# Operand sums taken pair by pair and one bank for the first half's products, in the output projection of a two-layer decoder

## The chip, the cores and the metric

The kernel runs on one core of a Trainium2 chip. The metric is the device time of one execution in microseconds. Each engine works through its own list of instructions in order. In the profile PE is TensorE's matmuls (PEld its weight loads), DVE is VectorE, ACT is ScalarE, POOL is GpSimd and SP is SyncE.

## The reference, cut to what matters

A batch of one, 512 tokens, a width of 1024. Layer 0 mixes with gated linear attention, layer 1 with stick-breaking attention over 16 heads of 64; each mixer and each MLP (1024 to 4096 to 1024, squared ReLU) is followed by a layer norm of `ALPHA * h + result`. All is float32. The change lies in layer 1's mixer:

```python
k, v  = split(h @ kv_w);  q = h @ sb_w_q[0]
# per head and block of 128 queries, strictly causal:
z     = q @ k.T * 64 ** -0.5
w     = sigmoid(z) * product of (1 - sigmoid(z)) over the keys between
o     = w @ v                        # 512 x 1024 over all heads
mix   = o @ sb_w_o[0]                # the output projection, 1024 x 1024
h     = layer_norm(ALPHA * h + mix)  # then MLP, then layer norm
```

## The kernel before, in words

**Precision.** A float32 operand X is split into `hi` (X rounded to fp32r, a copy on ScalarE) and `lo` (X minus hi, a subtract: the "lo split"). A product is three matmuls: hi·hi, hi·lo, lo·hi. `split_tile` (L70, L72) splits a 128x1024 weight tile, `put` (L98, L99) an activation. `on=nc.gpsimd` sends a lo split to GpSimd; without it VectorE makes it. `raw`, `d`, `k` and `q` are buffers that weight tiles arrive in; `unit()` gives a 128 x 4 x 512 tile, in the profile `T`.

**Layer 1.** The heads go by pairs, eight of them. While pair p's weights are turned (`turn`: transposes at L973, ScalarE copies `wt` at L978), the queries of pair p+1 (`queries`, L927 and L928) and the keys of pair p+2 are projected; then come pair p+1's `weights` (scores at L939, mask at L956, sigmoids at L960 and L961, a reversed scan on VectorE at L964), then pair p's `outputs` (L987: 28 matmuls over `wt` and the values `vs`, into one PSUM bank). The scan's result needs the values as differences of neighbouring rows: `differences(n)` makes them for half n of the heads, by shifted DMA copies and four VectorE subtracts (L904). `vs[0]` serves pairs 0 to 3.

**The output projection.** o is cut in four blocks: columns of pairs 0 to 3 are `o1` (T_5008 in the order lists), those of pairs 4 to 7 `o2`; each has two halves of 256 tokens, a11 and a21 (of `o1`), a12 and a22 (of `o2`). The product is made with seven products instead of eight, in a scheme of operand sums: `first` takes a11, `seventh` a11 - a21, `sixth` and `fifth` sums with a22, `third` a sum with a12, and b2 and b4 are multiplied with parts of `o2` itself (`o2h`, `o2l`). b1 to b7 are the blocks of `sb_w_o` and sums of them, the sums made by accumulating DMAs (`fetch`, L1009). Each product is two half-products (s = 0, 1), each 12 matmuls on one PSUM bank (L1035), and `add` reads a finished bank into the residual rows: four row tiles `h` (in the order lists h_1637 to h_1640) of two 512-wide halves; L167 is the first read of such a half (it scales h by ALPHA), L169 any later one. The first product and half of the seventh run while pair 7's weights are turned; the rest, `project()`, after pair 7's outputs. `finish` then takes the layer norm's statistics of each row tile as it is complete (L177, L182 to L184, L190), transposes it (L231) and splits it (L98, L99) for the first matmuls of the MLP (L93 to L95, there 256 wide).

**What sets the order.** Code order and priorities, through a scheduler; `keep_in_program_order` (`keep`) pins an instruction against others that are pinned on its engine. A tile's buffer is handed on when its last reader is through.

## Time and profile before

| | us |
|---|---|
| median of three runs (lowest, highest) | 1122.48 (1121.60, 1123.09) |
| the profiled execution's own time | 1122.67 |
| its span in the trace, 0.998 granted clock | 1121.0 |
| busy: PE, DVE, ACT, POOL | 1104.7, 822.5, 571.7, 159.3 |

The 1.67 us between span and execution's time lie outside the trace. A timeline row gives start, duration, engine, line, operation and tile, a count and, in brackets, how long the engine had been idle before and what ended that. The durations of neighbours overlap a little, so the pace of a run is read from the distance of two starts. Attention lies at about 600 to 741 us of the span, the rest of the output projection at 741 to 781, the second MLP from there to the end.

### The profile page before, as it was taken

The numbers are of one execution on the slowest core, as the hardware profiler recorded it, in microseconds if no ns is written. First come the engines' busy times: TensorE is split into PE (matmuls) and PEld (weight loads), VectorE is DVE, ScalarE is ACT, GpSimd is POOL, SyncE is SP. The second block draws the span as 40 slices with busy tenths as digits, with TensorE's granted clock in tenths as the row PEclk, the third lists the DMA queues.
The fourth block names the chain that finished last, engine by engine and source line by source line (L and its number), as shares of the span: only waits on it lengthen the run. The fifth ranks groups of instructions, "written<-read, shape, count | busy, mean of one in ns | idle before, by whom it ended". The sixth has DMA issues, their size and how long they took to land.

```text
span 1121.0 us, 14387 instructions
## 1 busy us (share of the span) xinstructions
PE 1104.7 (99%) x5503; PEld 914.5 (82%) x5503; DVE 822.5 (73%) x1028; ACT 571.7 (51%) x855; POOL 159.3 (14%) x183
## 2 busy tenths in 40 slices
PE   9999999999999999999999999988999999999997
PEld 7888888898888888888888787767988888888885
DVE  4588649958957856849898877698479767667677
ACT  4455437643533534535765667665545435336353
POOL 1011222200100100122313000251200000000222
PEclk9999999999999999999999999999999999999999
DMA  8441399492670760888745352414926815706773
GB/s 248 121 132 57 119 257 207 126 298 84 199 210 22 197 198 19 220 190 169 216 107 170 94 149 78 104 34 126 313 82 191 241 57 164 229 21 187 174 133 89
DMA packets 111352, 169.06 MB, mean 151 GB/s; under 512 B 13178, under 2 KB 38138, under 8 KB 111284
## 3 DMA queue, kind: packets, MB, share of 16 engines
q1 hardware_dynamic: 86228, 119.39, 32.7%
q0 software_dynamic: 22592, 44.04, 22.6%
q10 hardware_dynamic: 2464, 4.72, 1.1%
q8 instruction: 43, 0.70, 0.2%
q14 instruction: 25, 0.20, 0.1%
HBM read 162.89 MB, written 3.15 MB: 148 GB/s over the span
## 4 chain that ended last, share of the span: by engine, by line
PE 90%; DVE 6%; ACT 1%; issue 1%; POOL 0%; POOLq 0%; DVEq 0%; ACTq 0%
PE ps L355 29%; PE ps L93 17%; PE ps L94 17%; PE ps L95 17%; PE ps L796 3%; DVE lo L72 1%; PE ps L939 1%; PE ps L973 1%; DVE c L964 1%; DVE T L99 1%; PE ps L987 1%; DVE h L169 1%; PE ps L231 1%; DVE bst L177 1%; DVE h L167 0%
## 5 line engine op out<-in xcount | busy, mean ns | idle before, releaser
L355 PE MATMUL ps<-hi,T 128*128 128x512 f32 x1008 | 313.3, 390 | 0.1
L93 PE MATMUL ps<-T,hi 128*128 128x512 f32 (+1 forms) x776 | 290.7, 375 | 0.0
L94 PE MATMUL ps<-T,hi 128*128 128x512 f32 (+1 forms) x776 | 287.9, 371 | 2.2 <-DVE T L99 2.1
L95 PE MATMUL ps<-T,lo 128*128 128x512 f32 (+1 forms) x776 | 287.7, 371 | 0.0
L70 ACT ACTIVATE hi<-raw 128x1024 fp32r<-128x1024 f32 x128 | 135.5, 1061 | 169.4 <-PE ps L355 59.6
L72 DVE TENSOR_TENSOR lo<-raw,hi 128x1024 fp32r<-128x1024 f32 x125 | 151.8, 1221 | 95.2 <-ACT hi L70 94.9
L355 PEld LDWEIGHTS ps<-hi,T 128*128 128x128 f32 x1008 | 188.9, 188 | 40.1 <-DVE T L99 0.6
L70 ACT ACTIVATE hi<-B 128x1024 fp32r<-128x1024 f32 x118 | 124.4, 1059 | 172.0 <-PE ps L94 107.3
L72 DVE TENSOR_TENSOR lo<-B,hi 128x1024 fp32r<-128x1024 f32 x118 | 142.9, 1221 | 87.6 <-ACT hi L70 87.6
L355 PE MATMUL ps<-lo,T 128*128 128x512 f32 x504 | 196.1, 389 | 0.0
L94 PEld LDWEIGHTS ps<-T,hi 128*128 128x128 f32 x776 | 147.1, 190 | 26.0 <-DVE T L99 2.7
L95 PEld LDWEIGHTS ps<-T,lo 128*128 128x128 f32 x776 | 146.9, 189 | 24.8
L93 PEld LDWEIGHTS ps<-T,hi 128*128 128x128 f32 x776 | 146.7, 189 | 24.4 <-issue 1.0
L314 POOL DMA_DIRECT2D B<-in_mlp_w_down_dram x52 | 62.9, 1257 | 542.8 <-DMA B<-in_mlp_w_down_dram 386.7
L355 PEld LDWEIGHTS ps<-lo,T 128*128 128x128 f32 x504 | 94.6, 188 | 19.5
L169 DVE TENSOR_TENSOR h<-h,ps 128x512 f32<-128x512 f32 x114 | 77.3, 681 | 2.6 <-PE ps L355 2.2
L99 DVE TENSOR_TENSOR T<-s,T 128x1024 fp32r<-128x1024 f32 (+1 forms) x52 | 54.7, 1054 | 10.6 <-ACT T L98 10.6
L98 ACT ACTIVATE T<-s 128x1024 fp32r<-128x1024 f32 (+1 forms) x52 | 48.4, 935 | 21.2 <-DVE s L721 14.1
L964 DVE TENSOR_TENSOR_SCAN c<-r,c 128x384 f32<-128x384 f32 (+2 forms) x64 | 49.8, 829 | 3.5 <-ACT c L961 3.4
L93 PE MATMUL ps<-hi,T 128*128 128x512 f32 x128 | 51.4, 402 | 0.0
L719 ACT ACTIVATE s<-ps 128x512 f32<-128x512 f32 x64 | 38.0, 594 | 25.9 <-PE ps L95 25.2
L95 PE MATMUL ps<-hi,T 128*128 128x512 f32 x128 | 50.3, 393 | 0.0
(212 smaller groups left out, 1310.4 us busy)
## 6 DMA issues: line engine op xcount, KB each, us to landing
raw<-in_mlp_w_up_dram SPq DMA_DIRECT2D x64, 512.0 KB, 5.5
B<-in_mlp_w_down_dram SPq DMA_DIRECT2D x64, 512.0 KB, 5.6
B<-in_mlp_w_down_dram POOLq DMA_DIRECT2D x52, 512.0 KB, 7.8
raw<-in_gla_w_in_dram SPq DMA_DIRECT2D x20, 512.0 KB, 3.6
raw<-in_mlp_w_down_dram SPq DMA_DIRECT2D x16, 512.0 KB, 4.7
B<-in_gla_w_o_dram POOLq DMA_DIRECT2D x14, 512.0 KB, 7.8
raw<-in_kv_w_dram SPq DMA_DIRECT2D x12, 512.0 KB, 4.6
B<-in_gla_w_o_dram SPq DMA_DIRECT2D x8, 512.0 KB, 6.3
```

Of the source, the lines that this page charges most:

```text
L70: keep(nc.scalar.activation(hi, raw, AF.Copy))
L72: keep((on or nc.vector).tensor_tensor(lo, raw, hi.bitcast(F32), op=ALU.subtract))
L93: keep(nc.tensor.matmul(ps, lhsT=a[0], rhs=b[0], start=first, stop=False))
L94: keep(nc.tensor.matmul(ps, lhsT=a[0], rhs=b[1], start=False, stop=False))
L95: keep(nc.tensor.matmul(ps, lhsT=a[1], rhs=b[0], start=False, stop=last))
L98: keep(nc.scalar.activation(hi, ps, AF.Copy))
L99: keep((on or nc.vector).tensor_tensor(lo, ps, hi.bitcast(F32), op=ALU.subtract))
L169: nc.vector.tensor_tensor(h, h, ps, op=op)
L314: nc.gpsimd.dma_start(out=b.rearrange("p (a b) -> p a b", a=2), in_=weights(k, h, j), accum_op=ALU.add)
L355: nc.tensor.matmul(banks[s], lhsT=a(k, s)[x], rhs=b[k][y], start=opens and (k, x, y) == (0, 0, 0), stop=closes and (k, x, y) == (3, 1, 0), ...
L719: nc.scalar.activation(s2[:, f, :], pss[f], AF.Relu)
L964: nc.vector.tensor_tensor_scan(down, r[:, at][:, ::-1], down, 0.0, op0=ALU.mult, op1=ALU.add)
```

## The change

1. `differences(0)` issues the shifted copies as before, and hands back a function that issues the four subtracts; it is called after pair 1's queries.
2. The operand sums are made as each pair's output comes: `less` is a11 - a21 for all four pairs of `o1`, made after pair 3. Then `sums(k, o)` makes, from the PSUM bank of pair 4, 5 and 7 (from the copy in `o2` for pair 6), a21 as the difference o[HI] - a21 and a11 from it and `less`: two 128x256 operations on VectorE. The seventh operand is split from `less` in one go. The first two units of `o2h` are copied in pair 7's turn, and their lo part is made behind it.
3. `add` finds out itself whether a row half is read for the first time. First, sixth, fifth and third product are summed on one bank for each s (`ys`), the seventh and b4 on another (`us`), b2 on a third (`xs`): each s has 7 reads by VectorE where it had 10.
4. Of the lo splits and sums on GpSimd (b2, b6's first, b5's first, b3's first, `sixth`, `fifth`, `less(most)`) only the two of b2 stay there; the others are on VectorE, or gone.

The diff, cut to its core:

```diff
--- before.py
+++ after.py
...
             nc.gpsimd.dma_start(out=shifted[t][P - 1:P, :], in_=v[P - 2:P - 1, t, :])
             if t:
                 nc.gpsimd.dma_start(out=shifted[t][0:1, :], in_=v[P - 1:P, t - 1, :])
-        for t in range(NT):
-            nc.vector.tensor_tensor(v[:, t, :], v[:, t, :], shifted[t], op=ALU.subtract)
+
+        def subtract(keep=lambda ins: ins):
+            for t in range(NT):
+                keep(nc.vector.tensor_tensor(v[:, t, :], v[:, t, :], shifted[t], op=ALU.subtract))
+
+        return subtract
...
-    def add(s, banks, i, j, first=False, last=False, **how):
-        hs[2 * i + s].add(j, banks[s], first, last, ALU.subtract if j else ALU.add, **how)
+    seen = set()
+
+    def add(s, banks, i, j, last=False, **how):
+        hs[2 * i + s].add(j, banks[s], (i, j, s) not in seen, last, ALU.subtract if j else ALU.add, **how)
+        seen.add((i, j, s))
...
-    differences(0)
+    subtract = differences(0)
     ALL = [(j, j, NT) for j in range(NT)]
     pool = dict(on=nc.gpsimd)
-    ys, us, xs, zs, ws = ([None, None] for _ in range(5))
-    most, rest = slice(0, 3), slice(3, 4)
-
-    def less(ks, eng):
-        eng.tensor_tensor(a22[:, ks, :], a22[:, ks, :], a21[:, ks, :], op=ALU.subtract)
-
-    def flip(ks):
-        return minus(a11[:, ks, :], a22[:, ks, :], a11[:, ks, :])
+    ys, us, xs = ([None, None] for _ in range(3))
+    full = slice(0, 4)
+
+    def sums(k, o):
+        tt(a21[:, k, :], o[:, HI], a21[:, k, :], op=ALU.subtract)
+        minus(a11[:, k, :], o[:, HI], less[:, k, :])
 
     for p in range(NP):
         made = pairs[p].turn()
         take = lambda at: lambda n: [next(made, None) for _ in range(at.get(n, 0))]
         if p + 2 < NP:
             pairs[p + 1].queries()
-            if 0 < p < NT:
+            if p == 0:
+                subtract(keep)
+            elif p < NT:
                 hs[p].affine(vec, keep)
             pairs[p + 2].keys(take(TAKE))
         elif p + 1 < NP:
             pairs[p + 1].queries(take(FILL))
         else:
             mid = take(FILLS)
+
+            def then(n):
+                mid(n)
+                if n == 11:
+                    keep(nc.scalar.activation(o2h[:, 0:2, :], o2[:, 0:2, :], AF.Copy))
+
             run(STEPS, halves(first), b1, ys, closes=False, mid=mid)
-            run(STEPS[:4], halves(seventh), b7, us, mid=lambda n: mid(8 + n))
+            run(STEPS[:4], halves(seventh), b7, us, closes=False, mid=lambda n: then(8 + n))
         for _ in made:
             pass
-        if p == NP - 2:
-            o2h, o2l = unit(F32R), unit(F32R)
-            put(o2h[:, 0:2, :], o2l[:, 0:2, :], o2[:, 0:2, :], keep)
         if p < NP - 2:
             pairs[p + 1].weights()
             if p == 1:
-                differences(1)
-            ops = pairs[p].outputs(ALL)
-        else:
-            ops = pairs[p].outputs(LAST)
+                differences(1)()
+        if p == NP - 1:
+            tt(o2l[:, 0:2, :], o2[:, 0:2, :], o2h[:, 0:2, :].bitcast(F32), op=ALU.subtract)
+            put(o2h[:, 2, :], o2l[:, 2, :], o2[:, 2, :], keep)
+            sums(2, o2[:, 2, :])
+            for s in range(2):
+                add(s, ys, 0, 0)
+        ops = pairs[p].outputs(ALL if p < NP - 2 else LAST)
...
                 o2 = unit(F32)
                 a12, a22 = o2[:, :, LO], o2[:, :, HI]
-            if p < NP - 2:
-                nc.scalar.activation(o2[:, p - 4, :], ops, AF.Copy)
+            if p == NP - 1:
+                put(o2h[:, 3, :], o2l[:, 3, :], ops)
+            if p != NP - 2:
+                sums(p - 4, ops)
+            nc.scalar.activation(o2[:, p - 4, :], ops, AF.Copy)
+        if p == 3:
+            first = unit(F32R)
+            into(first, a11, full)
+            less = sbp.tile([P, 4, 256], F32, name="less")
+            tt(less, a11, a21, op=ALU.subtract)
...
             pairs[p + 1].weights()
-            less(most, nc.gpsimd)
-            keep(flip(most))
...
-            seventh = unit(F32R)
-            for h in range(2):
-                ks, sub = slice(2 * h, 2 * h + 2), chain().rearrange("p (a b) -> p a b", a=2)
-                tt(sub, a11[:, ks, :], a21[:, ks, :], op=ALU.subtract)
-                put(seventh[:, ks, LO], seventh[:, ks, HI], sub)
...
-    ahead_of = lambda u, a, ks: keep(nc.scalar.activation(u[:, ks, LO], a[:, ks, :], AF.Copy))
-
-    ahead_of(sixth, a11, most)
-    for s in range(2):
-        for i, j in ((0, 1), (1, 0), (1, 1)):
-            add(s, ys, i, j, True, keep=keep)
-    nc.gpsimd.tensor_tensor(sixth[:, most, HI], a11[:, most, :], sixth[:, most, LO].bitcast(F32), op=ALU.subtract)
...
-    into(sixth, a11, rest)
-    b6 += parts(b22[1])
-    into(fifth, a22, slice(0, 4), **pool)
-    for j in range(2):
-        add(0, us, 1, j)
+            seventh, o2h, o2l = unit(F32R), unit(F32R), unit(F32R)
+            into(seventh, less, full)
+
+    b6 = pieces(b22)
+    sixth, fifth = unit(F32R), unit(F32R)
+    into(sixth, a11, full)
+    into(fifth, a21, full)
...
-        run(LATER, whole(0), b2, ys, opens=False)
+        run(LATER, whole(0), b2, xs)
         for s in range(2):
-            add(s, ys, 0, 0, True, True)
+            add(s, xs, 0, 0, last=True)
+        b5s = pieces(b5)
+        run(STEPS, halves(sixth), b6, ys, False, False)
+        for s in range(2):
+            add(s, ys, 1, 0)
         minus(a12, a12, a11)
-        b5s = parts(b5[0], **pool) + parts(b5[1])
-        run(STEPS, halves(sixth), b6, zs, closes=False)
-        for s in range(2):
-            add(s, zs, 1, 0)
         third = unit(F32R)
-        into(third, a12, slice(0, 4))
-        run(STEPS, halves(fifth), b5s, zs, False, False)
-        add(0, zs, 1, 1, last=True)
-        add(1, zs, 1, 1)
-        b3 = pieces_512(sb_w_o[0], 512, 2, 512, **pool) + pieces_512(sb_w_o[0], 768, 2, 512)
+        into(third, a12, full)
+        add(0, us, 1, 1)
+        b3 = pieces_512(sb_w_o[0], 512, 4, 512)
+        run(STEPS, halves(fifth), b5s, ys, False, False)
+        add(0, ys, 1, 1, last=True)
+        add(1, ys, 1, 1)
         b4 = pieces(b22)
         for s in range(2):
-            run(STEPS[4 * s:4 * s + 4], halves(third), b3, zs, False)
-            add(s, zs, 0, 1, last=True)
+            run(STEPS[4 * s:4 * s + 4], halves(third), b3, ys, False)
+            add(s, ys, 0, 1, last=True)
             yield s
-        up0.extend(pieces_512(mlp_w_up[1], 0, 4, 0, keep=keep))
-        run(STEPS[4:], halves(seventh), b7, us)
+        up0.extend(pieces_512(mlp_w_up[1], 0, 2, 0, keep=keep))
+        run(STEPS[4:], halves(seventh), b7, us, closes=False)
         add(1, us, 1, 1, last=True)
-        add(1, us, 1, 0)
         yield ~0
-        run(STEPS[:4], whole(256), b4, ws)
-        add(0, ws, 1, 0, last=True)
+        up0.extend(pieces_512(mlp_w_up[1], 256, 2, 0))
+        run(STEPS[:4], whole(256), b4, us, False)
+        add(0, us, 1, 0, last=True)
...
-        run(STEPS[4:], whole(256), b4, ws)
-        add(1, ws, 1, 0, last=True)
+        run(STEPS[4:], whole(256), b4, us, False)
+        add(1, us, 1, 0, last=True)
         yield 3
...
```

**How the order moves** (in brackets the engine or DMA queue whose semaphore is waited for)**, place one: VectorE at the start of attention**, behind pair 0's scans: the subtracts on the values (T_4806 before, T_4805 now), a lo split of weights, and the lo part of pair 1's queries (L928 before, L932 now). Before:

```order
L904 TENSOR_TENSOR T_4806<-T_4806,d_5497 128x512 [waits DMASW7_49,DMASW2_49,DMASW0_49]
L904 TENSOR_TENSOR T_4806<-T_4806,d_5498 128x512 [waits DMASW6_49,DMASW4_49,DMASW1_49]
L904 TENSOR_TENSOR T_4806<-T_4806,d_5498 128x512 [waits DMASW5_49,DMASW0_49]
L72 TENSOR_TENSOR lo_5567<-raw_5563,hi_5565 128x1024 [waits DMAHW0_49]
L928 SCALAR_TENSOR_TENSOR q_5176<-ps_5151,q_5176 128x512 [waits Activation_49]
```

Now:

```order
L72 TENSOR_TENSOR lo_5712<-raw_5708,hi_5710 128x1024 [waits DMAHW1_49,PE_49,Activation_49]
L932 SCALAR_TENSOR_TENSOR q_5172<-ps_5147,q_5172 128x512 [waits Activation_49]
L906 TENSOR_TENSOR T_4805<-T_4805,d_5127 128x512 [waits DMASW6_49,DMASW4_49,DMASW0_49]
L906 TENSOR_TENSOR T_4805<-T_4805,d_5127 128x512 [waits DMASW7_49,DMASW5_49,DMASW1_49]
L906 TENSOR_TENSOR T_4805<-T_4805,d_5128 128x512 [waits DMASW4_49,DMASW3_49,DMASW2_49]
L906 TENSOR_TENSOR T_4805<-T_4805,d_5128 128x512 [waits DMASW6_49,DMASW5_49,DVE_49]
```

The queries' lo part stood behind three subtracts and a lo split, and stands behind a lo split; the four subtracts follow it.

**Place two: ScalarE and VectorE at pair 6.** ps_6243 (now ps_6247) is the bank of pair 5's output, L1099 (now L1116) its copy to `o2`; L978 (L982) are the `wt` copies that pair 6's outputs are made from, L98 the hi part of the seventh operand. ScalarE before:

```order
L961 ACTIVATE c_6236<-ps_6182 128x256
L1099 ACTIVATE T_6072<-ps_6243 128x512 [waits PE_49]
L978 ACTIVATE wt_6296<-ps_6298 128x4x128 [waits PE_49]
L98 ACTIVATE T_6271<-c_6272 128x2x256 [waits DVE_49,PE_49]
L978 ACTIVATE wt_6297<-ps_6307 128x4x128 [waits PE_49]
L98 ACTIVATE T_6271<-c_6276 128x2x256 [waits DVE_49]
```

Now:

```order
L965 ACTIVATE c_6240<-ps_6186 128x256
L1116 ACTIVATE T_6074<-ps_6247 128x512 [waits DVE_49,PE_49]
L982 ACTIVATE wt_6293<-ps_6295 128x4x128 [waits PE_49]
L98 ACTIVATE T_6456<-less 128x4x256 [waits PE_49]
L982 ACTIVATE wt_6294<-ps_6304 128x4x128 [waits PE_49]
L982 ACTIVATE wt_6293<-ps_6316 128x3x128 [waits PE_49]
```

The copy of pair 5's output waited for PE alone, and now for VectorE too; the two L98 halves that waited for VectorE are one. What VectorE holds there, the end of pair 6's scans and what is behind them, before:

```order
L964 SCALAR_TENSOR_TENSOR c_6228<-r_6227,c_6228 128x128
L964 SCALAR_TENSOR_TENSOR c_6236<-r_6235,c_6236 128x256 [waits Activation_49] x2
L1124 TENSOR_TENSOR c_6272<-T_5008 128x512 [waits DVE_49,PE_49]
L1124 TENSOR_TENSOR c_6276<-T_5008 128x512 [waits DVE_49,PE_49]
L99 TENSOR_TENSOR T_6271<-c_6272,T_6271 128x2x256 [waits Activation_49]
```

Now:

```order
L968 SCALAR_TENSOR_TENSOR c_6232<-r_6231,c_6232 128x128
L968 SCALAR_TENSOR_TENSOR c_6240<-r_6239,c_6240 128x256 [waits Activation_49]
L1068 TENSOR_TENSOR T_5008<-ps_6247,T_5008 128x256 [waits PE_49]
L968 SCALAR_TENSOR_TENSOR c_6240<-r_6239,c_6240 128x256 [waits Activation_49]
L1049 SCALAR_TENSOR_TENSOR T_5008<-ps_6247,less 128x256
L99 TENSOR_TENSOR T_6456<-less,T_6456 128x4x256 [waits Activation_49]
L932 SCALAR_TENSOR_TENSOR q_6336<-ps_6283,q_6336 128x512 [waits Activation_49]
```

The two subtracts for the seventh operand (L1124) are gone, and the two sums of pair 5 (L1068, L1049), which read the bank of ScalarE's copy, stand among the last scans.

**Place three: behind pair 7.** VectorE from the reads of the seventh product on; d, k and q are tiles of b6 and b5, T_6350 and T_6458 the lo half of `o2`, T_6399 and T_6571 the sixth operand. Before:

```order
L167 SCALAR_TENSOR_TENSOR h_1640<-h_1640,ps_6482 128x512 x2
L169 TENSOR_TENSOR h_1639<-h_1639,ps_6509 128x512 [waits DVE_49,PE_49]
L169 TENSOR_TENSOR h_1639<-h_1639,ps_6509 128x512 [waits DVE_49]
L72 TENSOR_TENSOR lo_6579<-d_6266,hi_6577 128x1024 [waits DMASW5_49,Activation_49]
L99 TENSOR_TENSOR T_6350<-ps_6543,T_6349 128x512 [waits Activation_49]
L1061 TENSOR_TENSOR T_6072<-T_6072,T_5008 128x256 [waits Activation_49]
L1042 SCALAR_TENSOR_TENSOR T_5008<-T_6072,T_5008 128x256 [waits DVE_49]
L1042 SCALAR_TENSOR_TENSOR T_6072<-T_6072,T_5008 128x4x256 [waits DVE_49]
L99 TENSOR_TENSOR T_6399<-T_5008,T_6399 128x256 [waits Activation_49]
L167 SCALAR_TENSOR_TENSOR h_1637<-h_1637,ps_6469 128x512 [waits PE_49]
```

Now:

```order
L167 SCALAR_TENSOR_TENSOR h_1637<-h_1637,ps_6461 128x512 [waits PE_49]
L72 TENSOR_TENSOR lo_6565<-d_6271,hi_6563 128x1024 [waits DMASW4_49,Activation_49]
L167 SCALAR_TENSOR_TENSOR h_1638<-h_1638,ps_6474 128x512 [waits PE_49]
L72 TENSOR_TENSOR lo_6569<-d_6272,hi_6567 128x1024 [waits DMASW5_49,Activation_49]
L167 SCALAR_TENSOR_TENSOR h_1639<-h_1639,ps_6501 128x512 [waits PE_49]
L1100 TENSOR_TENSOR T_6458<-T_6074,T_6457 128x1024 [waits Activation_49]
L99 TENSOR_TENSOR T_6458<-T_6074,T_6457 128x512 [waits Activation_49]
L99 TENSOR_TENSOR T_6458<-ps_6543,T_6457 128x512 [waits Activation_49]
L1068 TENSOR_TENSOR T_5008<-ps_6543,T_5008 128x256
L1049 SCALAR_TENSOR_TENSOR T_5008<-ps_6543,less 128x256
L1049 SCALAR_TENSOR_TENSOR T_6074<-T_6074,T_5008 128x4x256 [waits Activation_49]
L99 TENSOR_TENSOR T_6571<-T_5008,T_6571 128x4x256 [waits Activation_49]
```

Of first and seventh product eight reads (L167, L169; the list begins with the last four) stood ahead of the lo split of d_6266, and now three do; the lo split of d_6271, units 0 and 1 of `o2`'s lo (L1100) and the whole sixth operand have come in, and, further down, the fifth operand and the lo split of k_6372. GpSimd over the same stretch, before:

```order
L1061 TENSOR_TENSOR T_6072<-T_6072,T_5008 128x3x256 [waits Activation_49]
L1137 TENSOR_TENSOR T_6399<-T_5008,T_6399 128x3x256 [waits Activation_49]
L72 TENSOR_TENSOR lo_6568<-d_6265,hi_6566 128x1024 [waits DMASW4_49,PE_49,Activation_49]
L72 TENSOR_TENSOR lo_6628<-k_6381,hi_6626 128x1024 [waits DMASW6_49,Activation_49]
L99 TENSOR_TENSOR T_6400<-T_6072,T_6400 128x4x256 [waits DVE_49,Activation_49]
L1009 DMA d_6265<-in_sb_w_o_dram 128x2x512 [waits Pool_49]
L1009 DMA d_6266<-in_sb_w_o_dram 128x2x512 [waits DMASW5_49]
L72 TENSOR_TENSOR lo_6697<-raw_6693,hi_6695 128x1024 [waits DMAHW0_49,Activation_49]
```

Now:

```order
L1013 DMA k_6372<-in_sb_w_o_dram 128x2x512 [waits DMAHW2_49,PE_49]
L72 TENSOR_TENSOR lo_6388<-raw_6384,hi_6386 128x1024 [waits DMAHW7_49,PE_49,Activation_49]
L1013 DMA q_6373<-in_sb_w_o_dram 128x2x512 [waits DMAHW3_49,DVE_49]
L1013 DMA d_6271<-in_sb_w_o_dram 128x2x512 [waits DMASW4_49,DVE_49]
L1013 DMA d_6272<-in_sb_w_o_dram 128x2x512 [waits DMASW5_49,DVE_49]
```

Its lo splits and sums behind the second one of b2 are gone, and the accumulating transfers (L1009, now L1013) follow one another.

More of the change, by code (lines that the diff above doesn't have):

```diff
@@ L1097, in yoco_kernel @@
                 a12, a22 = o2[:, :, LO], o2[:, :, HI]
-            if p < NP - 2:
-                nc.scalar.activation(o2[:, p - 4, :], ops, AF.Copy)
+            if p == NP - 1:
[8 more added lines that the diff above has]
+            tt(less, a11, a21, op=ALU.subtract)
+        if p == NP - 3:
+            b1 = pieces_512(sb_w_o[0], 0, 4, 0)
+            b22 = wide()
+            fetch(b22, 1, 1)
+            fetch(b22, 0, 1, True)
         if p == NP - 2:
-            put(o2h[:, 2, :], o2l[:, 2, :], ops)
-            nc.scalar.activation(o2[:, 2, :], ops, AF.Copy)
             b7 = pieces(b22)
@@ L1108, in yoco_kernel @@
             b2 = pieces_512(sb_w_o[0], 512, 4, 0, **pool)
-            sixth, fifth = unit(F32R), unit(F32R)
             pairs[p + 1].weights()
-            less(most, nc.gpsimd)
-            keep(flip(most))
-        if p == 3:
-            first = unit(F32R)
-            into(first, a11, slice(0, 4))
-        if p == NP - 3:
-            b1 = pieces_512(sb_w_o[0], 0, 4, 0)
-            b22 = wide()
-            fetch(b22, 1, 1)
-            fetch(b22, 0, 1, True)
-            seventh = unit(F32R)
-            for h in range(2):
-                ks, sub = slice(2 * h, 2 * h + 2), chain().rearrange("p (a b) -> p a b", a=2)
-                tt(sub, a11[:, ks, :], a21[:, ks, :], op=ALU.subtract)
-                put(seventh[:, ks, LO], seventh[:, ks, HI], sub)
-    def parts(b, **how):
-        hi, lo = split_tile(b, 2, **how)
-        return [(hi[:, i, :], lo[:, i, :]) for i in range(2)]
-    ahead_of = lambda u, a, ks: keep(nc.scalar.activation(u[:, ks, LO], a[:, ks, :], AF.Copy))
-    ahead_of(sixth, a11, most)
-    for s in range(2):
-        for i, j in ((0, 1), (1, 0), (1, 1)):
-            add(s, ys, i, j, True, keep=keep)
-    nc.gpsimd.tensor_tensor(sixth[:, most, HI], a11[:, most, :], sixth[:, most, LO].bitcast(F32), op=ALU.subtract)
-    b6 = parts(b22[0], keep=keep, **pool)
-    put(o2h[:, 3, :], o2l[:, 3, :], ops)
-    nc.scalar.activation(o2[:, 3, :], ops, AF.Copy)
-    less(rest, nc.vector)
-    flip(rest)
-    into(sixth, a11, rest)
-    b6 += parts(b22[1])
-    into(fifth, a22, slice(0, 4), **pool)
-    for j in range(2):
-        add(0, us, 1, j)
+            seventh, o2h, o2l = unit(F32R), unit(F32R), unit(F32R)
[4 more added lines that the diff above has]
+    into(fifth, a21, full)
     h3T = Split()
```

## The prediction

> **What bounds the kernel now.** I read the page first: busy times, then the chain that ended last.
>
> ```profile
> PE 1104.7 (99%) x5503; PEld 914.5 (82%) x5503; DVE 822.5 (73%) x1028; ACT 571.7 (51%) x855; POOL 159.3 (14%) x183
> PE 90%; DVE 6%; ACT 1%; issue 1%; POOL 0%; POOLq 0%; DVEq 0%; ACTq 0%
> ```
>
> PE is busy for all but 16 us, and the change leaves its matmuls alone. What can be won is time in which PE waits, and the next view is the list of PE's waits, from 600 us on (total, times, longest):
>
> ```profile
> PE ps L1035 <- DVE h L169: 2.5, 2, 1.5
> PE ps L94 <- DVE T L99: 2.1, 1, 2.1
> PE ps L1035 <- DVE T L99: 2.0, 2, 1.6
> PE ps L987 <- ACT wt L978: 1.1, 1, 1.1
> PE ps L939 <- DVE q L928: 1.0, 1, 1.0
> ```
>
> These 8.7 us all lie in attention, the projection and the head of the second MLP. The third view gives busy time by windows (PE, PEld, DVE, ACT, POOL, then granted clock, DMA share, GB/s):
>
> ```profile
> 750.00:760.00 10.00, 6.42 (x26) 4.72 (x27) 10.00 (x10) 2.65 (x3) 8.08 (x5) 1.00 0.50 85
> 780.00:785.00 5.00, 4.23 (x22) 4.23 (x23) 4.24 (x8) 2.35 (x3) 1.11 (x2) 0.66 0.40 119
> 900.00:1000.00 100.00, 100.00 (x443) 82.81 (x442) 69.44 (x72) 41.44 (x46) 4.81 (x4) 1.00 0.43 124
> ```
>
> Three readings. At 750 to 760 VectorE has no free moment and PE 3.6: there VectorE is the bound. At 780 to 785 the granted clock is 0.66, which costs 5 x 0.34 = 1.7 us. And the MLP keeps PE full for 100 us, so an earlier arrival there comes out as an earlier end. I sum in order of time.
>
> **Term 1, the subtracts moved.** At the start of attention:
>
> ```profile
> 615.92 1.86 DVE L904 TENSOR_TENSOR T<-T,d 128x512 f32<-128x512 f32 x3
> 617.71 1.21 DVE L72 TENSOR_TENSOR lo<-raw,hi 128x1024 fp32r<-128x1024 f32 x1
> 618.84 0.68 DVE L928 SCALAR_TENSOR_TENSOR q<-ps,q 128x512 fp32r<-128x512 f32 x1
> 619.57 2.19 PE L939 MATMUL ps<-k,q 64*128 64x512 f32 x23 [0.99 <-DVE q L928]
> ```
>
> PE waits 0.99 for the queries' lo part, which stands behind three subtracts. Now one lo split is ahead of it: it ends near 615.9 + 1.13 + 0.68 = 617.7, and PE is there at 618.58. The wait goes: **-1.0**. The four subtracts follow (4 x 0.62, to about 620.1). Their reader, pair 0's outputs, comes a whole batch of 23 score matmuls (2.1 us) after 618.58, so about 620.7. This cover is thin: were it gone, the wait returns there. Bounds 0 to -1.0; I take -1.0.
>
> **Term 2, the sums read a PSUM bank that ScalarE copies.** Pair 6:
>
> ```profile
> 718.14 0.69 ACT L978 ACTIVATE wt<-ps 128x512 f32<-128x512 f32 x1
> 720.07 0.63 ACT L98 ACTIVATE T<-c 128x512 fp32r<-128x512 f32 x1 [1.25 <-DVE c L1124]
> 721.61 1.20 ACT L978 ACTIVATE wt<-ps 128x384 f32<-128x384 f32 x4
> 722.66 1.08 ACT L70 ACTIVATE hi<-raw 128x1024 fp32r<-128x1024 f32 x1
> 723.61 0.63 ACT L927 ACTIVATE q<-ps 128x512 fp32r<-128x512 f32 x1
> 722.14 3.35 PE L987 MATMUL ps<-wt,T 128*64 128x256 f32 x28 [1.12 <-ACT wt L978]
> 715.79 3.60 DVE L964 TENSOR_TENSOR_SCAN c<-r,c 128x384 f32<-128x384 f32 x6 [0.49 <-ACT c L961]
> 731.46 0.40 DVE L956 TENSOR_TENSOR ps<-ps,low 128x256 f32<-128x256 f32 x1
> 727.21 0.68 DVE L99 TENSOR_TENSOR T<-ps,T 128x512 fp32r<-128x512 f32 x1
> 727.92 0.60 ACT L1102 ACTIVATE T<-ps 128x512 f32<-128x512 f32 x1 [1.71 <-DVE T L99]
> ```
>
> Today ScalarE's list stalls 1.25 for the seventh operand's subtract, and PE waits 1.12 for `wt`. The subtract goes, but in the new order the copy of pair 5's output waits for VectorE's two 256-wide reads of the same bank, and these stand among the last scans, which end at 719.39. Behind the copy are queued all of pair 6's `wt` copies, for which PE waits. The last two rows show such a wait: the copy starts at 727.92, VectorE's read of that bank ended at 727.89. So: scans to 719.39, two reads of 0.32 to 0.40 give 720.15, then, from start to start, copy 0.48, `wt` 0.47, the hi part at 0.95 (722.66 to 723.61), `wt` 0.52 and 0.46: 723.03. Today the `wt` that PE waits for is there about 722.08. **+1.0**, bounds +0.4 (the scheduler's last scan runs behind the first read) to +1.6. For pairs 4 and 5 the same wait lies under key and query projections.
>
> The Trainium skill has this as a rule ("PSUM — Partial Sum Buffer", section "PSUM bank collisions raise a hardware error"): two engines may not touch one bank's quadrant in the same cycle, reads included, so a tool orders them; it speaks against this change, and the two rows agree with it. Were reads free to overlap, this term would be about zero and the sum 1.0 lower.
>
> **Term 3, behind pair 7.** From the end of pair 7's outputs to the first transposes of the new rows:
>
> ```profile
> 740.54 0.50 PE L1035 MATMUL ps<-hi,T 128*128 128x512 f32 x1
> 762.45 0.61 PE L1035 MATMUL ps<-hi,T 128*128 128x512 f32 x2
> 763.13 0.61 PE L1035 MATMUL ps<-hi,T 128*128 128x512 f32 x2
> 770.84 1.03 PE L231 MATMUL ps<-ident,h 128*128 128x128 f32 x8
> ```
>
> Nine half-products of 12 matmuls at 0.68 per three are 24.5 us, and they take 30.3: 5.8 us are lost, the 4.5 us of waits at L1035 and the restarts after them. VectorE is late, and this is why:
>
> ```profile
> 741.60 2.40 POOL L72 TENSOR_TENSOR lo<-d,hi 128x1024 fp32r<-128x1024 f32 x1
> 742.76 2.33 DVE L72 TENSOR_TENSOR lo<-d,hi 128x1024 fp32r<-128x1024 f32 x1
> 747.35 3.39 POOL L72 TENSOR_TENSOR lo<-k,hi 128x1024 fp32r<-128x1024 f32 x1 [3.35 <-ACT hi L70]
> 748.41 2.60 DVE L99 TENSOR_TENSOR T<-T,T 128x256 fp32r<-128x256 f32 x1
> 753.33 1.20 DVE L72 TENSOR_TENSOR lo<-q,hi 128x1024 fp32r<-128x1024 f32 x1
> 754.72 3.36 POOL L72 TENSOR_TENSOR lo<-raw,hi 128x1024 fp32r<-128x1024 f32 x1
> 755.05 4.12 DVE L99 TENSOR_TENSOR T<-T,T 128x1024 fp32r<-128x1024 f32 x1
> ```
>
> Each of the three long VectorE operations has both inputs in SBUF and runs while GpSimd makes a split; the same 128x1024 form takes 1.20 at 753.33, between two of GpSimd's. Excess: 2.33 - 1.21, 2.60 - 0.43 and 4.12 - 1.21, together 6.2 us. The new list has nothing of GpSimd's there.
>
> Does VectorE keep up with the splits that it takes over? I count its operations from the first read of the first product to the last read ahead of the first row tile's statistics, at 0.60 for a 512-wide one, 1.14 for a 1024-wide one, 0.65 for statistics, 0.35 for a 256-wide one:
>
> - before: 15 reads, 1 split of 512, 7 wide, 3 statistics, 3 of 256: 20.6 us;
> - now: 10 reads, 2 splits of 512, 13 wide, 3 statistics, 2 of 256: 24.7 us.
>
> ```profile
> 737.97 3.66 DVE L167 SCALAR_TENSOR_TENSOR h<-h,ps 128x512 f32<-128x512 f32 x6
> 765.60 0.69 DVE L169 TENSOR_TENSOR h<-h,ps 128x512 f32<-128x512 f32 x1
> 768.27 0.81 DVE L190 TENSOR_SCALAR h<-h,mv,rs 128x1024 f32<-128x1024 f32 x1 [1.01 <-POOL rs L184]
> ```
>
> Before, these 20.6 us took 28.2 (737.97 to 766.2): excess 6.2 and 1.4 of idling. Now they can start at about 737.1, as the sum at the scans' end is gone, and end at 761.8. PE, unhindered, reaches the transposes at 740.54 + 24.5 = 765.0; from the last read to the centred rows it takes 769.1 - 766.2 = 2.9. So VectorE would have to be through by 762.1: it is in time by 0.3. Within the stretch I walked the list in the same way: the lo of `o2`'s first units is ready about 0.5 before b2's product wants it, the sixth operand 0.8, the reads that release `ys` for the fifth 0.1. The loss falls from 5.8 to about 0.2: **-5.6**. With so little margin the bounds are -3.0 (three places each late by a wide operation, 1.14, less the slack) and -5.8. For these margins I add **+0.3** in all.
>
> **Term 4, the first gap of the MLP.**
>
> ```profile
> 780.77 0.38 PE L94 MATMUL ps<-T,hi 128*128 128x256 f32 x1 [2.05 <-DVE T L99]
> 780.08 0.64 DVE L99 TENSOR_TENSOR T<-c,T 128x512 fp32r<-128x512 f32 x1
> ```
>
> PE waits 2.05 for the lo part of the third row tile. In the new order one 512-wide read fewer stands ahead of that on VectorE: 0.6 less, of which I take **-0.5**, bounds +0.5 and -2.0.
>
> **Term 5, the clock.** The drop to 0.66 follows the 2.05 us gap; the gaps of 1.6 and 1.5 us at L1035 left the clock at 1.00. A gap of about 1.5 should not bring it: **-1.7**, bounds 0 and -1.7. By the Trainium skill ("TensorE: Matmul & The Clock Gate", section "What's actually happening") the clock is gated after an idle window of some 3.4 us that runs free of the program; by that no gap of 2 us would do it alone, which this trace does not bear out, or else the phase decides. That gives the first rival.
>
> **The sum**: -1.0 + 1.0 - 5.6 + 0.3 - 0.5 - 1.7 = -7.5, from the profiled execution's 1122.67 (0.2 above the median of the runs): **1115.2 us**.
>
> **Rivals.**
>
> - *The clock drops all the same.* The gap at the MLP's head stays, only shorter, and whether it falls into the gate's phase isn't to be seen before. Then term 5 is nothing: 1116.9.
> - *VectorE stays the bound.* Its margin is 0.3 us on 24.7, its list is in order, and several wide splits stand behind hi copies of ScalarE; 1.4 us of idling were there before and 13 wide operations have 13 such waits. If the idling grows to 4 us, the stretch wins 1.5 only, the gap and clock stay: 1122.67 - 1.5 = 1121.2, no change. Against it: ScalarE has 7.35 us free of ten at 750 to 760.
> - *Slower: VectorE's long operations aren't GpSimd's doing.* If something else there (the accumulating transfers, the buffers) stretches them, 6.2 us of excess stay on top of 24.7: it ends at 768.0 where it ended at 766.2, +1.8, and with 13 wide operations where 7 were, the excess grows in proportion, by 5: +6.8 at most. It decides once more than 4.4 us of excess remain. Midway, with terms 1 and 2 cancelling: 1126. Against it: the three long operations are just those under GpSimd's splits.
>
> **How the numbers follow.** Forecast 0.58, clock rival 0.25, no change 0.11, slower 0.06. Best end: terms at their good bounds, -1.0 + 0.4 - 5.8 - 0.8 - 1.7 = -8.9, and a little for the gap: 1113. The other end reaches over the clock rival to a stretch that wins 3.0: 1122.67 - 3.0 - 0.5 = 1119.2. Range **1112.8 to 1119.5**. The three runs lie 1.5 us apart, and 0.2%, 2.2 us, is the least that I take to be told from no change: faster 0.83, same 0.11, slower 0.06.
>
> **What would show it.** No wait of L943 for the queries. Ahead of pair 6's outputs (now L991) a wait of about 2 us, ScalarE's copy released by VectorE's L1049. No wait over 0.3 at the products (now L1039), VectorE's wide operations at 1.2 throughout 738 to 765, the last read ahead of the statistics by 762. A gap of 1.6 or less at L94, and a granted clock of 1.00 from 770 to 785. Wrong I am if wide operations of VectorE still take over 2 us with GpSimd idle, or if PE waits at L1039 in new places.

## The result, and the profile after

The changed kernel takes 1115.89 us (median of five runs, 1114.49 to 1118.16) where the kernel before takes 1122.48 (five runs, 1121.47 to 1123.09): a ratio of 0.9944, 95% interval 0.9929 to 0.9958. The forecast was 1115.2, range 1112.8 to 1119.5. The profiled execution is the median one: 1115.89, span 1114.2.

The profile page's busy times, then PE's waits from 600 us on (total, times, longest):

```profile
PE 1102.6 (99%) x5503; PEld 913.9 (82%) x5503; DVE 818.2 (73%) x1029; ACT 572.1 (51%) x853; POOL 145.4 (13%) x177
```

```profile
PE ps L991 <- ACT wt L982: 2.0, 1, 2.0
PE ps L94 <- DVE T L99: 1.7, 1, 1.7
```

Of five entries two are left. The 4.5 us at the products (L1035, now L1039) and the 1.0 us at the scores are gone, the gap at the MLP's head is 1.7, and the wait ahead of pair 6's outputs has grown from 1.1 to 2.05. The windows (PE, PEld, DVE, ACT, POOL, granted clock, DMA share, GB/s):

```profile
715.00:725.00 10.00, 7.95 (x51) 5.91 (x51) 5.48 (x10) 6.96 (x17) 2.91 (x2) 0.88 0.50 118
750.00:760.00 10.00, 10.00 (x46) 8.29 (x45) 9.51 (x11) 4.25 (x4) 0.00 (x0) 1.00 0.29 96
780.00:785.00 5.00, 5.00 (x46) 5.00 (x45) 3.78 (x4) 3.56 (x11) 1.70 (x2) 1.00 0.82 265
```

At 750 to 760 PE is full where it had 6.4 of 10 us. The clock that was 0.66 at 780 to 785 is 1.00 there, but at 715 to 725, where it was 1.00, it is now 0.88. The rows of PE's timeline at the places of the prediction's sum:

```profile
618.11 2.18 PE L943 MATMUL ps<-k,q 64*128 64x512 f32 x24
620.23 2.38 PE L991 MATMUL ps<-wt,T 128*64 128x512 f32 x16
721.60 4.61 PE L991 MATMUL ps<-wt,T 128*64 128x256 f32 x28 [2.05 <-ACT wt L982]
741.24 0.50 PE L1039 MATMUL ps<-hi,T 128*128 128x512 f32 x1
765.87 1.03 PE L231 MATMUL ps<-ident,h 128*128 128x128 f32 x8
775.44 0.39 PE L94 MATMUL ps<-T,hi 128*128 128x256 f32 x1 [1.70 <-DVE T L99]
```

Set against the same rows of before (pair 0's outputs began at 621.69, the others are quoted in the prediction), the lead of the changed kernel grows and shrinks along the way, and each step is a term:

| reached by PE | before | after | lead | this step | forecast |
|---|---|---|---|---|---|
| pair 0's outputs | 621.69 | 620.23 | 1.46 | -1.46 | -1.0 |
| pair 6's outputs, start | 722.14 | 721.60 | 0.54 | +0.92 | +1.0 |
| the products behind pair 7 | 740.54 | 741.24 | -0.70 | +1.24 | none |
| transposes of the new rows | 770.84 | 765.87 | 4.97 | -5.67 | -5.6 + 0.3 |
| the MLP's lo products | 780.77 | 775.44 | 5.33 | -0.36 | -0.5 |
| end of the span | 1121.0 | 1114.2 | 6.8 | -1.47 | -1.7 |

VectorE and ScalarE at the two places that decide, from their timelines:

```profile
738.18 1.22 DVE L72 TENSOR_TENSOR lo<-d,hi 128x1024 fp32r<-128x1024 f32 x1
749.81 1.21 DVE L72 TENSOR_TENSOR lo<-k,hi 128x1024 fp32r<-128x1024 f32 x1
754.40 2.36 DVE L72 TENSOR_TENSOR lo<-raw,hi 128x1024 fp32r<-128x1024 f32 x2
761.53 0.69 DVE L167 SCALAR_TENSOR_TENSOR h<-h,ps 128x512 f32<-128x512 f32 x1
718.16 0.40 DVE L1049 SCALAR_TENSOR_TENSOR T<-ps,less 128x256 f32<-128x256 f32 x1
718.65 0.60 ACT L1116 ACTIVATE T<-ps 128x512 f32<-128x512 f32 x1 [2.29 <-DVE T L1049]
```

The wide operations take 1.2 us throughout, and the last read ahead of the first row tile's last statistics ends at 762.2. At pair 6 ScalarE stands 2.29 us for VectorE's second read of the bank, with the `wt` copies queued behind.

### The profile page after: what moved, and what is told of

Same layout as the page of the kernel before. It is cut to its first block, busy times and chain, and to the rows that moved or that the text cites. A ratio compares the mean times of both kernels' runs of the same rounds, so it can differ in the third digit from the quotient of the medians.

```text
span 1114.2 us, 14380 instructions
## 1 busy us (share of the span) xinstructions
PE 1102.6 (99%) x5503; PEld 913.9 (82%) x5503; DVE 818.2 (73%) x1029; ACT 572.1 (51%) x853; POOL 145.4 (13%) x177
## 4 chain that ended last, share of the span: by engine, by line
PE 90%; DMA 5%; DVE 2%; issue 1%; POOL 1%; ACT 1%; SPq 0%; POOLq 0%; DVEq 0%; ACTq 0%
PE ps L355 28%; PE ps L93 16%; PE ps L94 16%; PE ps L95 16%; DMA B<-in_gla_w_o_dram 5%; PE ps L796 3%; PE ps L1039 3%; PE ps L991 2%; PE ps L977 2%; PE ps L943 2%; PE ps L231 1%; DVE bst L177 0%; DMA h<-in_x_dram 0%; POOL B L314 0%; PE ps L584 0%
## 5 line engine op out<-in xcount | busy, mean ns | idle before, releaser
L94 PE MATMUL ps<-T,hi 128*128 128x512 f32 (+1 forms) x776 | 287.4, 371 | 1.8 <-DVE T L99 1.7
L94 PEld LDWEIGHTS ps<-T,hi 128*128 128x128 f32 x776 | 146.4, 189 | 25.7 <-DVE T L99 2.3
L169 DVE TENSOR_TENSOR h<-h,ps 128x512 f32<-128x512 f32 x108 | 73.3, 681 | 2.7 <-PE ps L355 2.4
L98 ACT ACTIVATE T<-s 128x1024 fp32r<-128x1024 f32 (+1 forms) x52 | 48.4, 935 | 21.2 <-DVE s L721 14.1
```

What stands on the lines that cost most here:

```text
L94: keep(nc.tensor.matmul(ps, lhsT=a[0], rhs=b[1], start=False, stop=False))
L98: keep(nc.scalar.activation(hi, ps, AF.Copy))
L169: nc.vector.tensor_tensor(h, h, ps, op=op)
```

## The experiments

Three reasons were on trial: that GpSimd's splits had held up VectorE (against: that the six reads fewer, or the sums made earlier, brought the gain), that the bank wait is what pair 6 costs, and that the clock's drop hangs on a gap near 2 us. Each experiment changes one thing, but for the last, a version meant to be faster. "Pair 0 to MLP" below is the distance on PE from the start of pair 0's outputs to the first L94 matmul behind the gap: 159.08 us before (780.77 - 621.69), 155.21 after. It leaves out what an execution gained or lost ahead of attention.

### Four operations back on GpSimd

```diff
-    b6 = pieces(b22)
...
+    b6 = parts(b22[0], **pool) + parts(b22[1])
...
-    into(fifth, a21, full)
+    into(fifth, a21, full, **pool)
...
-        b5s = pieces(b5)
+        b5s = parts(b5[0], **pool) + parts(b5[1])
...
-        b3 = pieces_512(sb_w_o[0], 512, 4, 512)
+        b3 = pieces_512(sb_w_o[0], 512, 2, 512, **pool) + pieces_512(sb_w_o[0], 768, 2, 512)
```

> The changed kernel with four operations moved back to GpSimd: the lo splits of the first tiles of b6, b5 and b3, and of the fifth operand. VectorE's list from pair 7 to the first statistics is 4 x 1.14 = 4.6 us shorter than in the changed kernel (20.1 us). Theory (VectorE's operations with two inputs in SBUF stand still while GpSimd makes a split): some wide VectorE operations take 2.3 to 4.2 us again, PE waits 2 to 5 us in the products behind pair 7, the span grows by 2 to 5 us, to 1116 to 1119. Rival (the gain came from the six reads fewer; GpSimd only relieves VectorE): all wide operations take 1.2 us, no wait at the products, the span is the same or up to 0.5 us shorter.

Measured: 1123.11 us (1121.68 to 1124.32, ten runs), ratio to before 1.0006 (0.9997 to 1.0015). These four alone take the whole gain back; the profiled execution, the shortest of the ten, has a span of 1119.9, a little over the range, and the median of the spans is 1121.4. PE's waits from 600 us on, then rows of VectorE, GpSimd and PE:

```profile
PE ps L1039 <- DVE h L167: 5.1, 1, 5.1
PE ps L991 <- ACT wt L982: 2.1, 1, 2.1
PE ps L94 <- DVE T L99: 1.5, 1, 1.5
```

```profile
735.58 2.19 DVE L72 TENSOR_TENSOR lo<-d,hi 128x1024 fp32r<-128x1024 f32 x1
744.88 1.37 DVE L169 TENSOR_TENSOR h<-h,ps 128x512 f32<-128x512 f32 x2
747.65 7.69 DVE L99 TENSOR_TENSOR T<-T,T 128x1024 fp32r<-128x1024 f32 x1 [0.21 <-ACT T L98]
733.90 2.78 POOL L72 TENSOR_TENSOR lo<-d,hi 128x1024 fp32r<-128x1024 f32 x1 [7.30 <-ACT hi L70]
744.49 2.70 POOL L99 TENSOR_TENSOR T<-T,T 128x1024 fp32r<-128x1024 f32 x1 [7.81 <-ACT T L98]
748.65 3.32 POOL L72 TENSOR_TENSOR lo<-k,hi 128x1024 fp32r<-128x1024 f32 x1
751.01 3.25 POOL L72 TENSOR_TENSOR lo<-raw,hi 128x1024 fp32r<-128x1024 f32 x1
756.09 0.77 PE L1039 MATMUL ps<-hi,T 128*128 128x512 f32 x1 [5.12 <-DVE h L167]
```

The third operand's lo split on VectorE (747.65) takes 7.69 us: it stands through two of GpSimd's splits, and the read of the sixth product that PE waits for is queued behind it. The reads at 744.88, which have one input in PSUM, lie under a GpSimd operation too and take 1.37 for two, where the changed kernel's take 1.28 (747.42). The rival is out: by the count VectorE had 4.6 us less to do, and the time rose by 7.2.

### The same part of the change alone

The four operations moved to VectorE in the kernel before:

```diff
-    b6 = parts(b22[0], keep=keep, **pool)
+    b6 = parts(b22[0], keep=keep)
...
-    into(fifth, a22, slice(0, 4), **pool)
+    into(fifth, a22, slice(0, 4))
...
-        b5s = parts(b5[0], **pool) + parts(b5[1])
+        b5s = parts(b5[0]) + parts(b5[1])
...
-        b3 = pieces_512(sb_w_o[0], 512, 2, 512, **pool) + pieces_512(sb_w_o[0], 768, 2, 512)
+        b3 = pieces_512(sb_w_o[0], 512, 4, 512)
```

> The kernel before with one part of the change alone: the lo splits of the first tiles of b6, b5 and b3, and of the fifth operand, on VectorE; the twenty reads, the operand sums and the rest are those of before. Theory: no wide VectorE operation behind 741 us takes over 1.3 us; VectorE's list there is 20.6 + 4 x 1.14 = 25.2 us instead of 20.6 + 6.2 of standing still, so PE loses 3 to 4.5 us there instead of 5.8 (the sixth operand's last unit stands behind the fifth operand, 1.1 us), and the span is 1117 to 1120. Rival (GpSimd isn't the cause, VectorE just has too much to do): the long operations stay, VectorE gets 4.6 us more, and the span grows by 3 to 5 us, to 1124 to 1126.

Measured: 1119.10 us (1118.70 to 1119.66, seven runs), ratio 0.9973 (0.9962 to 0.9984), span 1117.4, in the range. PE's waits at the transposes, the MLP's head and the products, and one row of VectorE:

```profile
PE ps L231 <- DVE h L190: 2.2, 2, 2.1
PE ps L94 <- DVE T L99: 0.9, 1, 0.9
PE ps L1035 <- DVE T L99: 0.9, 2, 0.6
PE ps L1035 <- DVE h L169: 0.2, 1, 0.2
```

```profile
742.73 2.34 DVE L72 TENSOR_TENSOR lo<-d,hi 128x1024 fp32r<-128x1024 f32 x2
```

The pair of wide operations takes 2.34 where one alone took 2.33 beside GpSimd. The transposes begin at 767.41 instead of 770.84, so PE's loss in the products falls from 5.8 us to 2.4, below the 3 to 4.5 of the forecast. By the medians the move off GpSimd is worth 3.4 us by itself, half of the gain, though it gives VectorE 4.6 us more to do. That is a balance: the gap at L94 is 0.95 here and the clock behind it stays at 1.00, and a new wait of 2.07 us comes at the transposes of a later row tile (787.48). Ahead of that wait VectorE itself (L190, 786.61) stands 2.09 for GpSimd's L184, where it stands 1.01 in the row of 768.27 in the kernel before; GpSimd was issuing a transfer from 784.39 on.

### The six reads put back as work

```diff
+    def again(s, banks, n):
+        for _ in range(n):
+            tt(sbp.tile([P, S], F32, tag="r", bufs=3, name=nm("r")), hs[s].h[:, 0:512], banks[s], op=ALU.add)
...
                 add(s, ys, 0, 0)
+                again(s, ys, 2)
+            again(0, us, 1)
...
         add(1, us, 1, 1, last=True)
+        again(1, us, 1)
```

> The changed kernel with the six reads that the change took off VectorE put back as work alone: four more 512-wide reads of the first product's banks and two of the seventh's, into a scratch tile. Theory (behind pair 7 VectorE has no more than about 1.6 us of idle time and 0.3 us of margin): its list grows by 6 x 0.6 = 3.6 us, PE waits 1.5 to 3.3 us in the products or at the transposes, and the span grows by as much, to 1115.7 to 1117.5. Rival (the reads lie beside PE's products and cost nothing once GpSimd is out of the way): the span stays at 1114.2 within 0.5.

Measured: 1119.85 us (1118.70 to 1121.26, ten runs), ratio 0.9983 (0.9974 to 0.9992); span 1116.8. The spans of its runs go from 1116.6 to 1119.2 with a median of 1117.8, those of the changed kernel from 1112.8 to 1116.5 with a median of 1114.2. PE's waits behind pair 7, but for one of 0.3:

```profile
PE ps L1039 <- DVE T L1104: 2.0, 1, 2.0
PE ps L231 <- DVE h L190: 1.7, 2, 1.5
PE ps L94 <- DVE T L99: 0.3, 1, 0.3
```

The first wait is for the lo part of `o2`, which stands behind the reads; another 1.5 comes at a later row tile. The reads are not free: 3.6 us of work come out as 2.6 us of span between the profiled executions and 3.6 between the medians. That the 3.6 and the 3.6 agree may be chance, since the kernel before took 1121.50 beside these runs and 1122.48 beside those of the changed kernel; about 1 us is not resolved. VectorE had little margin, then, and the rival is out. Two halves: without GpSimd's blocking or without the reads alone, the list does not fit under PE's products, and together it does.

### ScalarE's copy ahead of VectorE's sums

```diff
-            if p != NP - 2:
+            if p == NP - 1:
                 sums(p - 4, ops)
             nc.scalar.activation(o2[:, p - 4, :], ops, AF.Copy)
+            if p < NP - 2:
+                sums(p - 4, ops)
```

> The changed kernel with one pair of statements swapped for pairs 4 and 5: ScalarE's copy of the output bank to o2 is written ahead of VectorE's two sums from that bank, so VectorE waits for ScalarE and not the other way round. Theory (the bank wait at pair 6 is a cost of the change, and the half clock that follows it comes from that gap): PE's 2.05 us wait ahead of pair 6's outputs goes, the 28 matmuls take 2.4 to 3.4 us instead of 4.61, the granted clock at 715 to 725 is 1.00, and the time falls by 2 to 3.3 us, to a span of 1111 to 1112. Rival (ScalarE's queue is the limit there, the wait would stay for the other wt copies and the seventh operand's hi part): the wait stays above 1 us and the span above 1113.

Measured: 1112.17 us (1111.59 to 1112.71, four runs), ratio 0.9912 (0.9895 to 0.9928); span 1109.9, better than the range. Rows of ScalarE, VectorE and PE at pair 6, and the window:

```profile
715.50 0.68 ACT L1116 ACTIVATE T<-ps 128x512 f32<-128x512 f32 x1
717.15 0.40 DVE L1068 TENSOR_TENSOR T<-ps,T 128x256 f32<-128x256 f32 x1
718.78 3.10 PE L991 MATMUL ps<-wt,T 128*64 128x256 f32 x28
715.00:725.00 10.00, 10.00 (x80) 8.23 (x80) 6.14 (x13) 8.16 (x19) 4.71 (x3) 1.00 0.56 131
```

The copy comes right behind the sigmoids, the sums follow it without a wait of their own, and the 2.05 us and the drop of the clock are gone. Pair 0 to MLP is 151.60 us, 3.6 less than after. The order of two readers of a bank, both of which were there in time, had cost that, 1.2 of it by the drop of the clock (see the changed kernel once more, below).

### The sums of pairs 4 to 6 made together

```diff
-            sums(2, o2[:, 2, :])
+            tt(a21[:, 0:3, :], a22[:, 0:3, :], a21[:, 0:3, :], op=ALU.subtract)
+            minus(a11[:, 0:3, :], a22[:, 0:3, :], less[:, 0:3, :])
...
-            if p != NP - 2:
-                sums(p - 4, ops)
+            if p == NP - 1:
+                sums(3, ops)
```

> The changed kernel with the operand sums of pairs 4, 5 and 6 made together from the copies in o2 behind pair 6 (two 128x768 operations) instead of pair by pair from PSUM. Theory (making them pair by pair gains nothing, and its one effect on PE is the wait of ScalarE's copy at pair 6): the 2.05 us wait ahead of pair 6's outputs is gone and the span falls by 2 to 3.3 us, to 1111 to 1112. Rival (spreading the sums is what keeps VectorE's list short behind pair 7): the list is later by about 1 us, PE waits there or at pair 7's transposes, and the span is 1113.5 or more.

Measured: 1112.36 us (1112.15 to 1113.23, four runs), ratio 0.9916 (0.9901 to 0.9931), span 1110.8, a little better than the range. PE has no wait at pair 6:

```profile
719.69 3.09 PE L991 MATMUL ps<-wt,T 128*64 128x256 f32 x28
```

Pair 0 to MLP is 151.61 us, the same as with the copies first. Making the sums pair by pair gains nothing, then; in the changed kernel all that it did to PE was the bank wait.

### The subtracts put back

```diff
-    subtract = differences(0)
+    differences(0)()
...
-            if p == 0:
-                subtract(keep)
-            elif p < NT:
+            if 0 < p < NT:
```

> The changed kernel with the four subtracts on the values issued right after the shifted copies, as before. Theory: PE waits 1.0 us for the queries' lo part at the start of attention again, the start of pair 0's outputs is 1.46 us later (620.23 to 621.69), and the span grows by about 1.5 us, to 1115.7. Rival (a wait in the middle of attention is swallowed later, since VectorE and ScalarE run ahead of PE): the wait is back, and the span is the same within 0.3 us.

Measured: 1116.29 us (1114.87 to 1118.27, four runs), ratio 0.9948 (0.9933 to 0.9963); span 1116.6. By the medians this is no difference from the changed kernel, whose runs lie 3.7 us apart. The trace tells more:

```profile
619.29 0.50 PE L943 MATMUL ps<-k,q 64*128 64x512 f32 x1
620.77 2.19 PE L943 MATMUL ps<-k,q 64*128 64x512 f32 x23 [0.98 <-DVE q L932]
622.89 1.40 PE L991 MATMUL ps<-wt,T 128*64 128x512 f32 x6
```

The 0.98 is back, and from the first score matmul to pair 0's outputs it is 3.60 us instead of 2.12: 1.48 lost. From that matmul to the L94 matmul (777.85 - 619.29 = 158.56, against 157.33 after) 1.2 of them remain. So it is carried to the MLP. The missing 0.3 lies at pair 6: here the clock is at 0.50 already when the gap ends (724.30 to 725.30), part of the drop falls into the gap, and the 28 matmuls take 4.32 instead of 4.61. The timing of whole runs does not resolve any of this.

### The changed kernel once more, for the clock

> The changed kernel once more, for the granted clock alone. Theory (whether a gap of about 2 us halves the clock depends on where it falls in time, not on its length alone): the waits are the same to 0.1 us, 2.05 ahead of pair 6's outputs and 1.7 at the MLP's head, and the clock may drop behind one, both or none of them; each drop costs 1.2 to 1.7 us. Rival (a gap over a threshold near 2 us always does it): the clock drops behind pair 6's gap again and nowhere else, and the span is 1114.2 within 0.3.

Measured: 1115.10 us, span 1113.4. Its window at pair 6 and its row there:

```profile
715.00:725.00 10.00, 7.93 (x57) 5.96 (x56) 5.88 (x10) 7.36 (x18) 2.50 (x2) 1.00 0.54 128
722.01 3.35 PE L991 MATMUL ps<-wt,T 128*64 128x256 f32 x28 [2.07 <-ACT wt L982]
```

The same program, the same gap (2.07), and no drop: the 28 matmuls take 3.35 instead of 4.61. The threshold rival is out. Pair 0 to MLP is 154.01 against 155.21, so a drop there costs 1.2.

### A version with a shorter gap at the MLP's head

On top of the copies first: the lo part of row tile 1, the second (first four units), is pinned on VectorE ahead of a lo split of the MLP's weights and of the statistics of row tile 2, and its transposes are written ahead of those statistics. The core of the edit:

```diff
+        yield ~1
+        hs[2].pin = True
         add(0, us, 1, 0, last=True)
+        hs[2].pin = None
         yield 2
-        yield ~1
-        up0.extend(pieces_512(mlp_w_up[1], 512, 4, 0))
+        up0.extend(pieces_512(mlp_w_up[1], 512, 4, 0, keep=keep))
...
-    late = finish(project(), vcols, hs, h3T, chain)
+    late = finish(project(), vcols, hs, h3T, chain, keep=keep)
```

> A version meant to beat both: the changed kernel with ScalarE's copies first for pairs 4 and 5, and with the lo part of the second row tile's first four units pinned on VectorE ahead of a lo split of MLP weights (and the second tile's transposes issued ahead of the third tile's statistics). Theory (the gap at the MLP's head is VectorE's order, a 1.2 us split and 0.6 us of statistics that nobody waits for yet stand ahead of it): the gap falls from 1.7 us to about 0.6, and the span is 1108.5 to 1109.3, against 1109.9 with the copies first alone. Rival (ScalarE's hi part, or the weights, set the gap): the gap stays above 1.3 us and the span at 1109.9.

Measured: 1111.70 us (1111.13 to 1112.90, four runs), ratio 0.9907 (0.9891 to 0.9924). The wait at L94 is 0.8, but the profiled span was 1111.2, over the range: that execution had waited 1.29 us at 207.35, far from the edit, where the one with the copies first waited 0.16. So both versions ran again side by side.

> The version with ScalarE's copies first and the lo part pinned ahead of the weights' lo split, beside the version with the copies first alone, on one chip. Theory (the gap at the MLP's head is shorter by 0.9 us and nothing is given back behind it): its runs lie 0.9 to 1.5 us below those of the other, at 1110 to 1111 us. Rival (the shorter gap is lost again or drowned in the executions' own spread): the two agree within 0.5 us.

> The version with the copies first alone, beside the one above. Theory: 1112.0 us within 0.6, as it was, and 0.9 to 1.5 us above the other. Rival: no difference beyond 0.5 us.

Measured: 1111.54 us (1111.49 to 1111.91, four runs, ratio 0.9905, 0.9889 to 0.9922) with the lo part first, 1112.42 (1111.54 to 1113.14, four runs, ratio 0.9912, 0.9897 to 0.9927) with the copies first alone. L94's row in the one and in the other:

```profile
770.83 0.39 PE L94 MATMUL ps<-T,hi 128*128 128x256 f32 x1 [0.82 <-DVE T L99]
```

```profile
772.00 0.38 PE L94 MATMUL ps<-T,hi 128*128 128x256 f32 x1 [1.71 <-DVE T L99]
```

The gap is 0.9 shorter, pair 0 to MLP is 150.59 against 151.61, and the medians differ by 0.9. The intervals of the two ratios overlap, so the timing alone would not carry it; the traces and the medians agree. The times themselves lie above the forecast of 1110 to 1111. That part of the gap was VectorE's order, as the theory had it; what holds the 0.8 that is left was not tested. By the medians this version is the fastest of all: 4.3 us under the changed kernel.

## Why the prediction was right, point by point

**Term 3, right in cause and size.** Forecast -5.6, measured -5.67. The two sides of it were each shown: the blocking by GpSimd (four operations back: +7.2 us on the medians; off it in the kernel before: -3.4) and the length of VectorE's list (3.6 us of work more: +2.6 to +3.6 of span). The operations counted are those that ran. But that the last read's end came at 762.2 where the count put it at 761.8 is luck: the list began at 735.87 and not at 737.1, and it idled for some 1.6 us that the sum left out. The first row of VectorE's list after, and the two rows of before that by their times account for most of its early start (no run tests it alone):

```profile
735.87 0.66 DVE L167 SCALAR_TENSOR_TENSOR h<-h,ps 128x512 f32<-128x512 f32 x1
728.61 1.84 POOL L1061 TENSOR_TENSOR T<-T,T 128x768 f32<-128x768 f32 x1 [1.26 <-ACT T L1102]
729.53 2.00 DVE L964 TENSOR_TENSOR_SCAN c<-r,c 128x512 f32<-128x512 f32 x1 [1.24 <-ACT c L961]
```

The same scan takes 1.21 at 731.78. Before, it had stood 0.8 us under one of GpSimd's sums, an operation more that GpSimd held up and that the term did not count. For the added +0.3 there was no need: no product waited, and the first row tile was centred at 765.01 (L190, 764.20 and 0.81), 0.9 ahead of its transposes.

On the mechanism the Trainium skill ("SBUF — State Buffer", section "SBUF: two separate sides") says that GpSimd and a VectorE operation with two inputs in SBUF hold a shared port one at a time, for a whole instruction, and the other stands still. The traces agree: before, VectorE's operations of 742.76 and 755.05 ended at 745.09 and 759.17, GpSimd's at 744.00 and 758.08, 1.09 later both times; the scan's end of 731.53 is 1.08 after GpSimd's 730.45; with four operations back on GpSimd it is 737.77 after 736.68 and 755.34 after 754.26. These distances are about what such an operation takes alone (1.2), as if each began when GpSimd was through.

**Term 2, right, and worse than its number.** Forecast +1.0, measured +0.92, with the wait and its releaser as described, ScalarE's L1116 behind VectorE's L1049. What the term left out is what such a gap may bring: see term 5. And the wait was not the price of the sums but of the order of two statements, as the two experiments on it show.

**Term 1, right in cause, too small.** Forecast -1.0, measured -1.46. The term took the idle time in PE's row, 0.99, for the loss. In the row of before a lone matmul in front of the gap shows 0.50 us (618.08 to 618.58), where 24 in a row take 2.18, 0.09 each. So 0.4 of those 0.50 are lost as well, and the gap costs 0.4 to 0.5 more than its bracket says. With the subtracts put back it is the same: 0.98 in the bracket, 1.48 lost.

**Term 4, right in cause.** Forecast -0.5, measured -0.36: the gap is 1.70, not 1.55, and a little over the 1.6 named as the sign. The lo part that PE waits for is that of the second row tile, not of the third as the term says: pinning the second one's shortened the gap. The split and the statistics that still stood ahead of it were shown to be worth another 0.9; that one read fewer brought the 0.36 was not tested by itself.

**Term 5 was right at its place and wrong as a whole.** The drop at the MLP's head went (-1.47 for the forecast -1.7). That the shorter gap is the reason agrees with ten gaps of 1.46 to 1.72 us in the traces, none of them with a drop; but of eight gaps near 2 us four had none either, so chance may have a part in it. And the prediction looked for a gap of 2 us only there, while its own term 2 foresaw one of about 2 us at pair 6, and the clock dropped behind that: +1.24 that stands in no term. The rival that the clock drops all the same was given a chance of 0.25, for the MLP's head. In the profiled execution the like of it happened at pair 6; in the other execution of the same program it did not.

So of the difference from the forecast (1115.89 - 1115.2 = +0.7), the drop is +1.24, term 5's remainder +0.23, term 4's +0.14; term 1 gives -0.46, the margin not needed -0.3, and terms 2 and 3 together -0.15. That the sum lands within 0.7 is in part luck: a drop that stands in no term is set off by two terms that were too cautious. The slower rival, that something other than GpSimd stretched VectorE's operations, is out: with GpSimd idle none took over 1.25.

## What to carry to other kernels

An engine that looks like free help can be the reason why its neighbour is late: before moving work to GpSimd, look whether VectorE's operations of two SBUF inputs are longer under GpSimd's spans than elsewhere, and count the whole list at the undisturbed price against the time that it has. Where two engines read one bank, write the one first whose queue feeds the engine that sets the end; here that order was worth 2.4 us, and 3.6 with the drop of the clock behind it. And when a sum contains a new gap on PE, price what gaps of that length do to the clock elsewhere in the same trace.
